# The opening of a two-layer trunk: a part's weight transfers ordered behind that part's last modulation row

## The chip, the cores and the metric

One core of one Trainium2 chip runs the whole program. The metric is the device time of one execution in microseconds (us); shown is the median over runs of the same kernel. The engines are TensorE (PE; PEld is its weight load), VectorE (DVE), ScalarE (ACT), GpSimd (POOL) and SyncE (SP), whose queue issues nearly all DMA transfers here.

## The reference

Two decoder layers on a sequence of 256 tokens with 2048 channels, in float32. Cut to what matters for this change:

```
cond = silu(c)
for l in range(2):
    mod = einsum('bd,de->be', cond, w_ada[l]) + b_ada[l]     # (1, 6 * 2048)
    sh_m, sc_m, gt_m, sh_f, sc_f, gt_f = six pieces of mod
    u = x * (1 + sc_m) + sh_m
    proj = u @ w_in[l]                                       # 4896 columns
    # sliding-window attention on one group of columns,
    # RWKV-7 delta rule on the others
    mix = concat(y_attn, y_rwkv) @ w_out[l]
    x = layer_norm(ALPHA * x + gt_m * mix)
    u = x * (1 + sc_f) + sh_f
    x = layer_norm(ALPHA * x + gt_f * swiglu(u))
```

So before the first projection can begin, the first two of the six modulation vectors of layer 0 have to be there: a product of one vector with 2048 x 4096 numbers of `w_ada`, that is 32 MB which are read once and used once.

## The kernel before, in words

The work of a layer is a mixer (input projection, attention, delta rule in four chunks of 64 tokens, output projection) and a feed-forward part. All weights are streamed from HBM. A float32 product is made of three matmuls: each weight tile `raw` is split into `hi` (a cast on ScalarE, L435) and `lo = raw - hi` (a subtraction on VectorE, L436), each input `u` into two halves as well, and hi x hi, hi x lo and lo x hi are summed. Weight tiles have 1024 columns in all and go through rings: four `raw`, three `hi`, two `lo` (`WB`).

*The opening* (some 150 us) is handled in five parts of 4, 4, 4, 2 and 2 of the 16 channel tiles of 128. For each part the generator `parts` (inside the last section of the kernel)

- streams 16 rows of `w_ada` through `ada_first`: row tiles `ast` of 128 x 1024 (512 KB; in the two small parts two rows of 256 KB share one), a ring of eight; VectorE multiplies each by a column of `cond` and adds it to `aacc` (L356 the first, L358 the others);
- sums `aacc` over its partitions in `ada_sums`: four transposes on TensorE (L327), a sum along the row on ScalarE for each (L331), and the bias on VectorE (`mods`, L334), once for the shift and once for the scale;
- makes the part's inputs in `make_u`: transposes of x (`xt`, L1372; TensorE L409), shift and scale on ScalarE (L413, L415), the low half on VectorE (L416);
- yields, and `front` runs `tstream` on the part's weight tiles: three kinds of columns (`rk`, `lb` and `acc`), matmuls L469 and L470 on `hi` and L471 on `lo`. The tiles come from `steps`, which issues the transfers (L427), the cast and the subtraction.

The opening uses one PSUM bank for transposes, so the sums and the transposes of x take turns. Later modulations (the other pieces of layer 0 and all of layer 1) are made beside the stream: `ada_steps` issues their rows through two buffers, adds them on VectorE (L268, L270) or multiplies them on TensorE (L290), and ends in an L327 too.

The order in which each engine runs its instructions is not that of the source: a planner simulates the program and lists the instructions of each engine by its own clock, subject to the data dependences and to hand-made order dependences that wait for nothing on the chip (`order`, `tc.add_manual_dep`: the second stands behind the first in the list). Within an engine everything then runs strictly in that list's order. All transfers are issued from SP's list; each waits there for the transfer eight before it, and for its buffer.

`lead` holds the name of the row transfer that `ada_first` issued last. It serves two helpers, `fetch` and `setup`, which put small parameter transfers behind it.

Of the kernel before, what the change touches and what calls it, by code (L numbers as in the profile page):

```python
# [69 lines left out]
def hybrid_trunk_kernel(  # L70
# [9 lines left out]
    dma = nc.sync.dma_start  # L80
# [11 lines left out]
    def bank(name="mb", tag="mb"):  # L92

        if tag == "cb":
            return ps.tile([P, 512], F32, tag="cb", name=name)
        t = f"m{turn[0]}"
        turn[0] ^= turn[1]
        return ps.tile([P, 512], F32, tag=t, name=name, bufs=1)
# [49 lines left out]
    order = mybir.DependencyInfo(mybir.DependencyClass.NoSync, mybir.DependencyReason.DATA)  # L148
# [23 lines left out]
    def fetch(dst, src, later=True):  # L172
        ins = dma(dst, src)
        if later:
            tc.add_manual_dep(ins.ins, lead[0], order, reason="behind the first modulation rows")
# [164 lines left out]
            S.copy(row, rb[0:n, 0:P])  # L340
            dma(gates[l, mod // 3, c0 // P:c0 // P + n], row)

    lead = []

    def ada_first(pool, c0, w):

# [36 lines left out]
    def pump():  # L383

        pace[1] += pace[0]
        while pace[1] >= 1.0:
            pace[1] -= 1.0
            next(ada_rest, None)
# [5 lines left out]
    def md(l, mod, kt, n=1):  # L394
        return mods[l][:, mod * KT + kt:mod * KT + kt + n]
# [23 lines left out]
    def steps(srcs, W, kts, room=None, off=0):  # L419


        no = max(1, 1024 // W)
        for i0 in range(0, len(kts), no):
            m = min(no, len(kts) - i0)
            raw = wp.tile([P, 1024], F32, tag="raw", name="raw", bufs=WB[0])
            for dst, src in srcs(raw[:, 0:m * W].rearrange("p (k w) -> p k w", w=W), kts[i0], m):
                dma(dst, src)  # L427
            if room:
                parts = [(raw[:, o * W:(o + 1) * W], *room()) for o in range(m)]
            else:  # L430
                hi = wp.tile([P, 1024 + WPAD], F32R, tag="hi", name="hi", bufs=WB[1])[:, off:off + 1024]
                lo = wp.tile([P, 1024 + WPAD], F32R, tag="lo", name="lo", bufs=WB[2])[:, off:off + 1024]
                parts = [(raw[:, 0:m * W], hi[:, 0:m * W], lo[:, 0:m * W])]
            for fl, h, r in parts:
                S.copy(h, fl)  # L435
                ins = V.tensor_tensor(r, fl, h.bitcast(F32), ALU.subtract)  # L436
            anchor[:] = [ins.ins.name]
            for o in range(m):
                if room:
                    yield i0 + o, *parts[o][1:]  # L440
                else:
                    yield i0 + o, hi[:, o * W:(o + 1) * W], lo[:, o * W:(o + 1) * W]
            pump()
# [42 lines left out]
    def cols(w, c0, width):  # L486
        wv = w.rearrange("(k p) n -> p k n", p=P)

        def f(rv, k0, m):
            return [(rv, wv[:, k0:k0 + m, c0:c0 + width])]  # L490
        return f
# [26 lines left out]
    def front(l, us, feeds, ahead=False):  # L518

        lb = [bank("lb", "cb") for _ in range(2)]  # L520
        vb = [acc_ps.tile([P, 512], F32, tag="acc", name="acc") for _ in range(4)]
        lblocks = [(0, 128, lb[0][:, 0:T], True, False), (128, 128, lb[0][:, T:2 * T], False, True),
                   (256, 32, lb[1][0:32, 0:T], not ahead, not ahead)]
        vblocks = [((2 * q + i) * P, P, vb[q][:, i * T:(i + 1) * T], i == 0, i == 1) for q in range(4) for i in range(2)]
        rk = None
        if ahead:
            b = ps.tile([P, 512], F32, tag="m1", name="rk0", bufs=1)
            turn[:] = 0, 0
            rk = [[b[:, 0:T], b[:, T:2 * T]], [lb[1][:, T:2 * T], None]]
            rblocks = [(0, P, rk[0][0], True, False), (P, P, rk[1][0], True, True), (2 * P, P, rk[0][1], False, True)]  # L530
            wrk = w_in[l][:, R0:R0 + 2 * RW].rearrange("(k p) (s n) -> p k s n", p=P, s=2)

            def rk_cols(rv, k0, m):
                return [(rv[:, :, 0:T], wrk[:, k0:k0 + m, 0, 0:T]), (rv[:, :, T:T + P], wrk[:, k0:k0 + m, 1, 0:P])]
        for kts, _ in feeds:
            fl = dict(first=kts[0] == 0, last=kts[-1] == KT - 1)
            if ahead and kts[0] == 0:
                tstream(rk_cols, T + P, kts, us, rblocks, **fl)
            tstream(cols(w_in[l], LORA0, 288), 288, kts, us, lblocks, **fl)
            if ahead and kts[0] > 0:  # L540
                tstream(rk_cols, T + P, kts, us, rblocks, **fl)
            tstream(cols(w_in[l], R0 + 2 * RW, RW), RW, kts, us, vblocks, **fl)
        return lb, vb, rk
# [814 lines left out]
    with tc.tile_pool(name="pro", bufs=1) as pp:  # L1358
        xv = x[0].rearrange("(t p) d -> p t d", p=P)

        def parts():
            k0 = 0
            for n in PARTS:
                o, w = k0 * P, n * P
                xt = pp.tile([P, 2, 512], F32, tag="xt", name="xt", bufs=2)[:, :, 0:w]
                side = setup(pp, 0, 0) if k0 == 0 else iter(())
                rows = ada_first(pp, o, w)
                for j in range(512 // w, KT + 1, 512 // w):
                    next(rows)
                    next(side, None)  # L1370
                    if j == 8:
                        dma(xt, xv[:, :, o:o + w])  # L1372
                for _ in side:
                    pass
                for _ in rows:
                    pass
                kts = list(range(k0, k0 + n))
                make_u(pp, [xt[:, 0, :], xt[:, 1, :]], k0, lambda kt: md(0, 1, kt), lambda kt: md(0, 0, kt), us, kts, IDLE["first"] if k0 + n == KT else 0)
                k0 += n
                yield kts, (0, 1)  # L1380
            for l, half in ((0, 1), (1, 0), (1, 1)):
                for _ in setup(pp, l, half, lead):
                    pass
            rope(pp)
            zt = pp.tile([P, 520], F32, name="zt")
            G.memset(zt, 0.0)
            for t in tinv:
                fetch(t.rearrange("e s t -> (e s t)").rearrange("(p n) -> p n", p=P), zt)
        feeds = front(0, us, parts(), ahead=True)
    for l in range(L):  # L1390
        pace[0] = AP[l]
        with tc.tile_pool(name=f"mix{l}", bufs=1, reuse_waits="tile") as mp:
            ys, wa = mixer(l, us, mp, feeds)
        pace[0] = AO[l]
        with tc.tile_pool(name=f"ffn{l}", bufs=1, reuse_waits="tile") as fp:
            us, feeds = channel(l, ys, wa, fp)
# [30 lines left out]
```

## Time and profile before

| | |
|---|---|
| median of 3 runs | 2643.07 us (2640.19 to 2645.76) |
| the profiled execution by its own time | 2641.74 us |
| its span | 2640.0 us |
| TensorE busy in the span | 2499.2 us (95%) |
| VectorE busy | 1803.9 us (68%) |
| ScalarE busy | 1185.9 us (45%) |
| the opening's rows and weights (issued before 128 us) | 46.50 MB at a mean of 363 GB/s |

How to read the profile's lines. In the timeline each line is a start, a duration, an engine, a source line, the operation, output <- inputs with their shapes, a count, and in brackets how long the engine stood idle before it and what ended that. In the table by stretches each engine has its busy time (with its count), then the granted TensorE clock (1.00 is full), the mean busy share of the core's 16 DMA engines and the rate in GB/s.

### The profile page before, as it was taken

How to read it: one execution, taken by the hardware profiler on the slowest of the kernel's cores; microseconds unless marked ns; L12 is line 12 of the kernel's file. 1: busy time of each engine (PE TensorE's matmuls, PEld its weight loads, DVE VectorE, ACT ScalarE, POOL GpSimd, SP SyncE). 2: the span in 40 equal slices, each digit the busy share in tenths (PEclk: the TensorE clock that was granted, in tenths of full speed). 3: DMA queues.
4: the chain of work that ended last, by engine and by line, in shares of the span. 5: the costliest groups of instructions: out<-in, count | busy, mean ns of one | idle time of the engine just before them, and what ended most of it. 6: DMA issues, size and time to landing. Idle time of an engine off the chain costs nothing.

```text
span 2640.0 us, 42213 instructions
## 1 busy us (share of the span) xinstructions
PE 2499.2 (95%) x15619; PEld 2081.6 (79%) x15619; DVE 1803.9 (68%) x2439; ACT 1185.9 (45%) x2023; POOL 144.1 (5%) x368
## 2 busy tenths in 40 slices
PE   3799998999999999999999989989899999999997
PEld 3797785677888888888898977867788888888887
DVE  7977666579877787777887776565755455545456
ACT  2464454435544444444454545544444443344442
POOL 1002222000000000000000024110000000000000
PEclk9899999999999999999999999989999999999999
DMA  9988667698998888888878784415665655566654
GB/s 371 343 267 256 195 187 250 224 357 290 339 329 307 312 314 312 287 311 296 300 240 282 219 262 147 130 51 210 211 199 186 191 188 193 194 190 190 191 188 147
DMA packets 336383, 637.50 MB, mean 241 GB/s; under 512 B 59510, under 2 KB 126514, under 8 KB 334642
## 3 DMA queue, kind: packets, MB, share of 16 engines
q1 hardware_dynamic: 333170, 629.05, 71.1%
q0 software_dynamic: 1280, 2.62, 0.4%
q10 hardware_dynamic: 1728, 3.15, 0.3%
q8 instruction: 122, 2.00, 0.3%
q14 instruction: 83, 0.68, 0.1%
HBM read 622.08 MB, written 12.62 MB: 240 GB/s over the span
## 4 chain that ended last, share of the span: by engine, by line
PE 80%; DMA 10%; DVE 7%; issue 2%; ACT 1%; SPq 0%; POOL 0%; DVEq 0%; ACTq 0%; POOLq 0%
PE acc L458 21%; PE acc L457 20%; PE acc L460 20%; DMA ast<-in_w_ada_dram 5%; PE acc L471 2%; PE acc L469 2%; PE acc L470 2%; DVE lo L436 2%; DMA raw<-in_w_in_dram 1%; DVE aacc L270 1%; DMA raw<-in_w_out_dram 1%; DVE aacc L358 1%; PE mb L1296 1%; PE mb L327 1%; PE gv L290 1%
## 5 line engine op out<-in xcount | busy, mean ns | idle before, releaser
L436 DVE TENSOR_TENSOR lo<-raw,hi 128x1024 fp32r<-128x1024 f32 (+2 forms) x728 | 881.3, 1211 | 556.7 <-PE acc L458 378.2
L435 ACT CAST hi<-raw 128x1024 fp32r<-128x1024 f32 (+2 forms) x728 | 758.2, 1044 | 1051.8 <-PE acc L460 831.0
L458 PE MATMUL acc<-lo,u 128*128 128x512 f32 x1568 | 514.8, 396 | 8.5 <-DVE lo L436 8.5
L460 PE MATMUL acc<-hi,u 128*128 128x512 f32 x1568 | 508.1, 393 | 0.0
L457 PE MATMUL acc<-hi,u 128*128 128x512 f32 x1568 | 460.0, 395 | 2.0 <-ACT sg L1289 1.2
L270 DVE SCALAR_TENSOR_TENSOR aacc<-ast,cond,aacc 128x1024 f32<-128x1024 f32 x270 | 344.9, 1277 | 39.5 <-DMA ast<-in_w_ada_dram 39.0
L458 PEld LDWEIGHTS acc<-lo,u 128*128 128x128 f32 x1568 | 295.2, 189 | 71.6 <-DVE lo L436 10.9
L457 PEld LDWEIGHTS acc<-hi,u 128*128 128x128 f32 x1568 | 296.1, 189 | 65.1 <-ACT sg L1289 1.6
L460 PEld LDWEIGHTS acc<-hi,u 128*128 128x128 f32 x1568 | 296.7, 189 | 61.7
L458 PE MATMUL acc<-lo,ht 128*128 128x512 f32 (+1 forms) x720 | 243.3, 377 | 1.6 <-DVE lo L436 1.6
L460 PE MATMUL acc<-hi,ht 128*128 128x512 f32 (+1 forms) x720 | 242.2, 375 | 0.0
L457 PE MATMUL acc<-hi,ht 128*128 128x512 f32 (+1 forms) x720 | 217.0, 376 | 0.0
L469 PE MATMUL acc<-u,hi 128*128 128x256 f32 x720 | 201.5, 287 | 1.9 <-ACT hi L435 1.9
L470 PE MATMUL acc<-u,hi 128*128 128x256 f32 x720 | 200.5, 286 | 0.0
L471 PE MATMUL acc<-u,lo 128*128 128x256 f32 x720 | 189.9, 290 | 7.1 <-DVE lo L436 6.9
L458 PEld LDWEIGHTS acc<-lo,ht 128*128 128x128 f32 x720 | 135.1, 188 | 27.0 <-DVE lo L436 3.1
L460 PEld LDWEIGHTS acc<-hi,ht 128*128 128x128 f32 x720 | 135.6, 188 | 24.3
L457 PEld LDWEIGHTS acc<-hi,ht 128*128 128x128 f32 x720 | 134.8, 188 | 24.3
L469 PEld LDWEIGHTS acc<-u,hi 128*128 128x128 f32 x720 | 139.9, 194 | 5.8 <-ACT hi L435 2.3
L470 PEld LDWEIGHTS acc<-u,hi 128*128 128x128 f32 x720 | 139.5, 194 | 2.8 <-issue 1.7
L471 PEld LDWEIGHTS acc<-u,lo 128*128 128x128 f32 x720 | 131.2, 194 | 12.1 <-DVE lo L436 9.0
L1135 POOL TENSOR_TENSOR brs<-brs,mhalf 128x1 f32<-128x1 f32 x8 | 6.2, 785 | 1687.4 <-DVE brs L1134 766.8
(358 smaller groups left out, 2900.7 us busy)
## 6 DMA issues: line engine op xcount, KB each, us to landing
ast<-in_w_ada_dram SPq DMA_DIRECT2D x368, 512.0 KB
raw<-in_w_gate_up_dram SPq DMA_DIRECT2D x704, 256.0 KB
raw<-in_w_down_dram SPq DMA_DIRECT2D x176, 512.0 KB
raw<-in_w_in_dram SPq DMA_DIRECT2D x82, 512.0 KB
raw<-in_w_out_dram SPq DMA_DIRECT2D x64, 512.0 KB
raw<-in_w_in_dram SPq DMA_DIRECT2D x120, 256.0 KB
ast<-in_w_ada_dram SPq DMA_DIRECT2D x32, 256.0 KB
lnw<-in_ln_w_dram SPq DMA_DIRECT2D x4, 1024.0 KB
```

Source lines behind the costliest of these rows:

```text
L270: ins = V.scalar_tensor_tensor(acc, t, cond[:, j:j + 1], acc, ALU.mult, ALU.add)
L290: PE.matmul(gv[32 * q:32 * q + 32, 0:T], lhsT=cond[:, j:j + 1].to_broadcast([P, 32]), rhs=t[:, q * T:(q + 1) * T], start=(j == 0), stop=(j ...
L327: PE.transpose(b[:, i * P:(i + 1) * P], blocks[q + i], ident)
L358: V.scalar_tensor_tensor(acc, t[:, j], cond[:, j0 + j:j0 + j + 1], acc, ALU.mult, ALU.add)
L435: S.copy(h, fl)
L436: ins = V.tensor_tensor(r, fl, h.bitcast(F32), ALU.subtract)
L457: PE.matmul(bt, lhsT=xh, rhs=hi[:, c0:c0 + w], start=st, stop=False)
L458: PE.matmul(bt, lhsT=xh, rhs=lo[:, c0:c0 + w], start=False, stop=False)
L460: PE.matmul(banks[t][q][:, 0:w], lhsT=xl, rhs=hi[:, c0:c0 + w], start=False, stop=sp_)
L469: PE.matmul(bt, lhsT=hi[:, c0:c0 + w], rhs=xh, start=st and opens, stop=False)
L470: PE.matmul(bt, lhsT=hi[:, c0:c0 + w], rhs=xl, start=False, stop=False)
L471: PE.matmul(bt, lhsT=lo[:, c0:c0 + w], rhs=xh, start=False, stop=sp_ and closes)
```

## The change

The weight transfers that `steps` issues while the opening is built get an order dependence on `lead[0]`, the last row transfer of the part that is in hand. A flag, `opening`, is true around the call of `front` that builds the opening and false afterwards. No instruction, no byte and no wait is added; the planner's lists change.

```
--- before.py
+++ after.py
-    lead = []
+    lead, opening = [], [False]
...
             for dst, src in srcs(raw[:, 0:m * W].rearrange("p (k w) -> p k w", w=W), kts[i0], m):
-                dma(dst, src)
+                ins = dma(dst, src)
+                if opening[0]:
+                    tc.add_manual_dep(ins.ins, lead[0], order, reason="behind the modulation rows of the part")
...
+        opening[0] = True
         feeds = front(0, us, parts(), ahead=True)
+        opening[0] = False
```

What moves is seen in the lists. Lines behind L427 are two higher after the change (L436 becomes L438, L469 to L471 become L471 to L473), those in the last section more.

The first place is SP's list in part 0. `ast` are rows, `raw` weights, `xt` a piece of x, `posi` the positions; the part's last row is ast_213. Before:

```order
L353 DMA ast_195<-in_w_ada_dram 128x2x512
L427 DMA raw_268<-in_w_in_dram 128x2x256
L353 DMA ast_198<-in_w_ada_dram 128x2x512
L427 DMA raw_268<-in_w_in_dram 128x2x128
L427 DMA raw_293<-in_w_in_dram 128x2x256
L353 DMA ast_201<-in_w_ada_dram 128x2x512
L427 DMA raw_293<-in_w_in_dram 128x2x128
L427 DMA raw_318<-in_w_in_dram 128x3x288
L353 DMA ast_204<-in_w_ada_dram 128x2x512
L427 DMA raw_351<-in_w_in_dram 128x288
L1372 DMA xt_486<-in_x_dram 128x2x512
L353 DMA ast_207<-in_w_ada_dram 128x2x512
```

The same place after the change, from the row transfer ast_204 on:

```order
L353 DMA ast_204<-in_w_ada_dram 128x2x512
L353 DMA ast_207<-in_w_ada_dram 128x2x512
L353 DMA ast_210<-in_w_ada_dram 128x2x512
L353 DMA ast_213<-in_w_ada_dram 128x2x512
L427 DMA raw_268<-in_w_in_dram 128x2x256
L427 DMA raw_268<-in_w_in_dram 128x2x128
L427 DMA raw_293<-in_w_in_dram 128x2x256
L427 DMA raw_293<-in_w_in_dram 128x2x128
L427 DMA raw_318<-in_w_in_dram 128x3x288
L427 DMA raw_351<-in_w_in_dram 128x288
L353 DMA ast_488<-in_w_ada_dram 128x2x512
```

The six weight transfers stand behind all sixteen rows, and the next part's first row (ast_488) behind them; on VectorE the subtractions of raw_268 and raw_293 likewise moved from between the rows to behind them. Over the whole opening the same transfers stand ahead of the last row.

The second place is VectorE's list where part 2's rows end and part 3's begin (aacc_1129, row pairs ast_1130, ast_1135, ...); lo_750 and lo_780 are weight tiles of part 1. Before:

```order
L358 SCALAR_TENSOR_TENSOR aacc_808<-ast_855,cond_131,aacc_808 128x1024
L356 TENSOR_SCALAR aacc_1129<-ast_1130,cond_131 128x2x256
L358 SCALAR_TENSOR_TENSOR aacc_1129<-ast_1130,cond_131,aacc_1129 128x2x256
L436 TENSOR_TENSOR lo_750<-raw_747,hi_749 128x1024
L334 SCALAR_TENSOR_TENSOR mods0_127<-asum_858,par0_123 128x4
L358 SCALAR_TENSOR_TENSOR aacc_1129<-ast_1135,cond_131,aacc_1129 128x2x256
L436 TENSOR_TENSOR lo_780<-raw_777,hi_779 128x1024
```

And after:

```order
L358 SCALAR_TENSOR_TENSOR aacc_808<-ast_855,cond_131,aacc_808 128x1024
L438 TENSOR_TENSOR lo_750<-raw_747,hi_749 128x1024
L356 TENSOR_SCALAR aacc_1129<-ast_1130,cond_131 128x2x256
L438 TENSOR_TENSOR lo_780<-raw_777,hi_779 128x1024
L358 SCALAR_TENSOR_TENSOR aacc_1129<-ast_1130,cond_131,aacc_1129 128x2x256
L334 SCALAR_TENSOR_TENSOR mods0_127<-asum_858,par0_123 128x4
```

The two weight tiles moved ahead of row work of part 3, as their transfers did on SP ahead of ast_1130's pair.

The third place is TensorE's list at the end of the opening, where the rows of part 4 end: mb_1353 are the transposes of its sums (aacc_1310), hi_1070 and lo_1071 a weight tile of part 2. Before:

```order
L469 MATMUL acc_155<-u_892,hi_1040 128x256
L470 MATMUL acc_155<-u_892,hi_1040 128x256
L471 MATMUL acc_155<-u_892,lo_1041 128x256
L327 MATMUL mb_1353<-ident_75,aacc_1310 128x128 x2
L469 MATMUL acc_152<-u_902,hi_1070 128x256
L470 MATMUL acc_152<-u_902,hi_1070 128x256
L469 MATMUL acc_153<-u_902,hi_1070 128x256
```

And after:

```order
L473 MATMUL acc_155<-u_892,lo_1041 128x256
L471 MATMUL acc_152<-u_902,hi_1070 128x256
L472 MATMUL acc_152<-u_902,hi_1070 128x256
L471 MATMUL acc_153<-u_902,hi_1070 128x256
L472 MATMUL acc_153<-u_902,hi_1070 128x256
L471 MATMUL acc_154<-u_902,hi_1070 128x256
L472 MATMUL acc_154<-u_902,hi_1070 128x256
L471 MATMUL acc_155<-u_902,hi_1070 128x256
L472 MATMUL acc_155<-u_902,hi_1070 128x256
L327 MATMUL mb_1353<-ident_75,aacc_1310 128x128 x2
L473 MATMUL acc_152<-u_902,lo_1071 128x256
```

The eight matmuls on hi_1070 moved ahead of the transposes; those on lo_1071 stay behind them. Further on in the same list the transposes of part 4's x (L409, mb_1366) moved from 40 weight matmuls ahead of the first matmul that uses their result (u_1373) to directly ahead of it.

In the mixer of layer 0 the lists differ as well. Weight matmuls stand 20 to 70 places earlier against the operations of the delta rule; between one pair of L806 groups of its inversion there are 28 weight matmuls now and 60 before. The rows of aacc_3833 (a later modulation) begin two weight tiles later on VectorE, and behind the subtraction lo_5601 nine of the sixteen are left, against seven before. From layer 0's feed-forward part on the lists are nearly the same.

## The prediction

> **What bounds the kernel now.** I read the page's engine table and chain first, then a table by stage, then the timeline of the opening, because the edit acts there and nowhere else by itself.
>
> ```profile
> span 2640.0 us, 42213 instructions
> PE 2499.2 (95%) x15619; PEld 2081.6 (79%) x15619; DVE 1803.9 (68%) x2439; ACT 1185.9 (45%) x2023; POOL 144.1 (5%) x368
> PE 80%; DMA 10%; DVE 7%; issue 2%; ACT 1%; SPq 0%; POOL 0%; DVEq 0%; ACTq 0%; POOLq 0%
> ```
>
> TensorE is busy for 2499.2 of 2640.0 us, so only the 141 us in which it stands idle can be won. The stages, with PE, PE weight loads, DVE, ACT and POOL busy time, then the granted clock, the DMA share and GB/s:
>
> ```profile
> 20.00:40.00 20.00, 2.31 (x9) 1.51 (x10) 15.49 (x28) 5.65 (x21) 0.00 (x0) 1.00 1.06 392
> ...
> 30.00:58.00 28.00, 18.18 (x120) 16.15 (x121) 24.46 (x38) 9.48 (x29) 0.00 (x0) 1.00 1.04 392
> 58.00:94.00 36.00, 27.01 (x204) 25.67 (x204) 34.67 (x37) 13.70 (x32) 0.00 (x0) 0.89 1.06 392
> 94.00:128.00 34.00, 25.69 (x192) 23.40 (x190) 31.50 (x50) 17.64 (x45) 0.00 (x0) 0.90 0.99 325
> ...
> 160.00:260.00 100.00, 94.23 (x842) 83.74 (x842) 79.78 (x127) 52.43 (x107) 18.63 (x35) 0.95 0.83 262
> 360.00:460.00 100.00, 87.78 (x931) 62.93 (x930) 77.26 (x169) 44.66 (x121) 17.38 (x39) 0.95 0.82 259
> ```
>
> From 20 to 128 us DMA (0.99 to 1.06 of its engines) and VectorE (90.63 of 98 us from 30 to 128) are both full, TensorE is not. After 160 TensorE is the bound, with stalls of some us in the mixer. So the question is whether anything gained in the opening reaches 128 us, and what the new order does to the mixer.
>
> **The change part by part.** No instruction and no byte is added. First the modulation rows of part 0, which now go ahead of that part's six weight transfers (2 of 256 KB, 2 of 128 KB, 432 KB, 144 KB: 1344 KB). The timeline of before:
>
> ```profile
> 29.90 1.28 DVE L358 SCALAR_TENSOR_TENSOR aacc<-ast,cond,aacc 128x1024 f32<-128x1024 f32 x1 [1.85 <-DMA ast<-in_w_ada_dram]
> ...
> 34.32 1.12 PE L327 MATMUL mb<-ident,aacc 128*128 128x128 f32 x4 [19.06 <-DVE aacc L358]
> ...
> 39.90 0.16 DVE L334 SCALAR_TENSOR_TENSOR mods<-asum,par 128x4 f32<-128x4 f32 x1 [0.86 <-ACT mb L331]
> ...
> 42.13 0.42 DVE L416 TENSOR_TENSOR u<-uf,u 128x256 fp32r<-128x256 f32 x1 [0.87 <-ACT u L415]
> 42.15 0.58 PE L469 MATMUL rk<-u,hi 128*128 128x256 f32 x1 [1.11 <-ACT u L415]
> ...
> 112.56 0.94 DVE L436 TENSOR_TENSOR lo<-raw,hi 128x768 fp32r<-128x768 f32 x1
> ```
>
> 1344 KB are 1.376 MB; at 392 GB/s (the 20:40 row) that is 3.5 us. The last rows wait for DMA (1.85 us at 29.90), so they end 3.5 us sooner, and two subtractions of 0.94 us each (the last row above is of that shape) no longer stand between them. The transposes then begin at about 30.6 instead of 34.32. From there to the first matmul took 42.15 - 34.32 = 7.8 us; ACT now has a cast or two of the moved weights in between (1.04 us for a wider one, at 124.40 below), so I give it 8.4 to 9.0, and the first matmul comes at 39.0 to 39.6: 2.6 to 3.2 us sooner. The moved weights land 3.5 us behind the last row, near 32.5, well ahead of that. VectorE has the same work behind it at its first L416 and fewer waits, so it too is up to 2.8 us ahead.
>
> Does that last? TensorE is idle a quarter of the time until 128, so it needs rows, and rows need DMA and VectorE. The last wait of VectorE before the end of the opening is this:
>
> ```profile
> 96.58 1.22 DVE L436 TENSOR_TENSOR lo<-raw,hi 128x1024 fp32r<-128x1024 f32 x1 [1.88 <-ACT hi L435]
> 96.60 0.58 PE L469 MATMUL acc<-u,hi 128*128 128x256 f32 x1 [1.85 <-ACT hi L435]
> ...
> L353 SPq DMA_DIRECT2D ast<-in_w_ada_dram x80: 367/368/748, 1.3 to 117.0; - x80
> ```
>
> At 96.58 VectorE and TensorE wait together for a weight tile's cast, that is for a landing. In the new order that tile stands one row pair (512 KB, 1.3 us at 392 GB/s) further ahead and the row pair behind it: by 96.6 the same bytes must have come in. VectorE then reaches 96.6 with its work changed by one pair against one tile (1.23 against 1.22 us), and from there to 129.20 it has no gap over 0.2 us. So I take the head start as eaten here: 0. The bounds are -2.8 us (all kept: the last row was issued at 117.0 and used 10 us later, so the ring would allow it) and +1.0 (a row pair waited for where a tile was).
>
> Second, the end of the opening. Rows of before, then TensorE in two stretches:
>
> ```profile
> 123.39 4.68 DVE L358 SCALAR_TENSOR_TENSOR aacc<-ast,cond,aacc 128x512 f32<-128x512 f32 x6
> ...
> 124.40 1.04 ACT L435 CAST hi<-raw 128x1024 fp32r<-128x1024 f32 x1 [2.88 <-DMA raw<-in_w_in_dram]
> ...
> 127.98 1.22 DVE L436 TENSOR_TENSOR lo<-raw,hi 128x1024 fp32r<-128x1024 f32 x1
> ...
> 128.21 0.66 PE L327 MATMUL mb<-ident,aacc 128*128 128x128 f32 x2 [3.93 <-DVE aacc L358]
> ...
> 130.38 0.41 PE L471 MATMUL acc<-u,lo 128*128 128x256 f32 x1
> ...
> 142.12 0.60 PE L409 MATMUL mb<-ident,xt 128*128 128x128 f32 x4
> ...
> 143.57 0.56 ACT L415 ACTIVATE u<-mb,mods 128x256 fp32r<-128x256 f32 x1
> ```
>
> ```profile
> 130.00:135.00 5.00, 5.00 (x29) 5.00 (x29) 2.16 (x4) 1.94 (x5) 0.00 (x0) 0.62 0.89 265
> 135.00:140.00 5.00, 5.00 (x46) 4.96 (x45) 1.62 (x2) 0.03 (x1) 0.00 (x0) 1.00 1.00 367
> ```
>
> Before, TensorE stood 3.93 us for the transposes of part 4's sums although hi_1070 was cast by 125.44; its eight matmuls came behind, until 130.38. Now those eight stand ahead of the transposes. lo_1071 is ready at 127.98 + 1.22 = 129.20, so the first L471 comes at 129.20, not 130.38: -1.2 us. The idle time falls into two pieces, 1.4 us until 125.4 and 1.7 us from 126.3 to 128.0. After 3.93 us the clock was 0.62, and 29 matmuls went in 5 us where 46 go at full clock: 17 x 5/46 = 1.85 us lost. What gaps do to the clock here:
>
> ```profile
> 63.84 0.39 PE L471 MATMUL acc<-u,lo 128*128 128x256 f32 x1 [2.73 <-DVE lo L436]
> ...
> 93.66 1.09 PE L327 MATMUL mb<-ident,aacc 128*128 128x128 f32 x4 [2.96 <-DVE aacc L358]
> ```
>
> ```profile
> 93.00:96.00 3.00, 1.09 (x4) 0.72 (x4) 1.66 (x3) 1.13 (x5) 0.00 (x0) 0.50 1.09 366
> 62.00:65.00 3.00, 1.16 (x9) 1.17 (x10) 3.00 (x4) 1.04 (x1) 0.00 (x0) 1.00 1.07 390
> ```
>
> A gap of 2.73 us left the clock at 1.00, one of 2.96 us was followed by 0.50. Two gaps of 1.4 and 1.7 us should leave it whole: between 0 and -1.85; I take -1.5, since 0.7 us of waiting for lo_1071 could come near enough to join the two. The Trainium skill ("TensorE: Matmul & The Clock Gate", Part 1: The HAM clock gate) has the array drop to half rate after an idle window of about 3.4 us, and ask as long a busy one to return. The gap of 2.96 us speaks for a shorter limit here; by the page's figure this term would be an estimated -1.7, by the rows it is -1.85, so the sum hardly depends on which holds.
>
> Against it, the transposes of part 4's inputs (L409, 142.12) had 40 weight matmuls between them and the first use of their result; now that use follows at once. The result was ready at 143.57 + 0.56 = 144.13, and L409 ended at 142.72: +1.4 us, with bounds 0 (if the weights are late anyway) and 1.4. Opening: -1.2 - 1.5 + 1.4 = -1.3, between -5.9 (all of the head start and of the clock, and no L409 wait) and +2.4 (the bad bound of the head start, neither gain).
>
> Third, the mixer of layer 0. The planner places weight matmuls 20 to 70 earlier against the chain of the delta rule, and row work of the later modulations later. Rows of before:
>
> ```profile
> 375.79 0.39 PE L457 MATMUL acc<-hi,u 128*128 128x512 f32 x1
> 376.01 0.39 PE L458 MATMUL acc<-lo,u 128*128 128x512 f32 x1
> ...
> 388.90 0.67 DVE L814 TENSOR_TENSOR tm<-tm,m 128x512 f32<-128x512 f32 x1
> ...
> 391.83 0.69 DVE L802 STREAM_TRANSPOSE ytr<-tm 128x512 f32<-128x512 f32 x1
> ...
> 399.70 1.28 DVE L270 SCALAR_TENSOR_TENSOR aacc<-ast,cond,aacc 128x1024 f32<-128x1024 f32 x1
> ...
> 412.83 1.28 DVE L270 SCALAR_TENSOR_TENSOR aacc<-ast,cond,aacc 128x1024 f32<-128x1024 f32 x1 [2.38 <-DMA ast<-in_w_ada_dram]
> ...
> 415.84 1.09 PE L327 MATMUL mb<-ident,aacc 128*128 128x128 f32 x4 [5.28 <-DVE aacc L270]
> ```
>
> One step of the inversion (L813 to the next L806) loses its weight matmuls: 0.67 + 0.69 = 1.4 us uncovered, 2.7 if a row of 1.28 us is ahead in VectorE's queue. At 415.84 TensorE waits 5.28 us for a sum whose last rows come one per (412.83 - 399.70)/4 = 3.3 us, by DMA. Behind the last weight tile of that stretch seven of them were left, now nine: +6.6 us if that tile comes no sooner, about 0 if it comes 7 us sooner: 32 of its matmuls, 0.22 us apart (375.79, 376.01), that now run before one step of the inversion instead of behind it. The other way, more weights ahead of the chain means its inputs are older when it reads them: the idle time of the two stages quoted above, 5.8 and 12.2 us, could shrink; I allow -4. Between -4 and 6.6 + 1.4 = +8 I take +1.5, near the step that surely loses its cover, and count the row wait as mostly absorbed in the 5.28 us that are waited already. The feed-forward stages keep their order: 0.
>
> The sum is -1.3 + 1.5 = +0.2 us. The profiled run took 2641.74 us by its own time (1.7 more than its span) and lies 1.3 under the median 2643.07; the shift is applied to the median: **2643.3 us**.
>
> **The rivals.** *The head start is kept (faster).* VectorE is 2.8 us ahead at its first L416 and never pays it back, so 128.21 becomes 125.4 and the clock stays up. For it: the last row was issued 10 us before its use. Against it: the wait at 96.58. Opening -1.2 - 1.85 - 2.8 + 1.4 = -4.5, and the mixer at -2 instead of +1.5: 2636.6.
>
> *The sums of the next modulation come late (slower).* Two rows more behind the last weight tile, 3.3 us each, at the L327 that already waits 5.28 us; it decides when that wait passes 5.28 + 1.5. With the uncovered step: -1.3 + 6.6 + 1.4 = +6.7: 2649.8. For it: rows there come by DMA alone. Against it: earlier weight tiles start the rows' clock earlier.
>
> *Weights come too late to their matmuls (slightly slower).* A part's tiles behind its rows would be missed at each hand-over as at 96.60, 1.85 us; if the last parts repeat it once more at 128 and the order gains nothing: +1.4 + 1.85 = +3.3: 2646.4. In part 0 the tiles have some 6 us to spare. The Trainium skill ("Trainium Kernel Development and Optimization", Best Practices) advises double buffering so that transfers overlap compute, which speaks against fetching weights later; in this trace transfers overlap in either order, DMA being full.
>
> *Nothing lasting happens:* head start and tail both vanish, 2643.
>
> **How the numbers follow.** About 0.2%, 5.3 us, is what a measurement of this kernel can tell from no change. Forecast 0.44 (its own range 2638 to 2648), kept head start 0.22, late sums 0.20, late weights 0.08, nothing 0.06. Faster by over 5.3 us needs 2637.8: most of the kept head start (0.18) and an edge of the forecast (0.04), 0.22. Slower needs 2648.4: most of the late sums (0.18), some of the late weights and of the forecast's edge (0.05), 0.23. The rest is 0.55. The range reaches from the kept head start, 2636, to the late sums with the opening's bad bound, 2652.
>
> **What would show it.** Right: part 0's transposes near 30.6 and first matmul near 39.3; VectorE and TensorE together near 96 and 128 as before; the eight hi_1070 matmuls before the L327 at 128; full clock from 130 to 135; an idle of about 1.4 us behind the last L409. Wrong: the L327 at 126 or sooner, the clock still near 0.62, the wait of the L327 at 415.84 over 7 us, or other stalls in the mixer that move the end by over 5 us.

## The result and the profile after

| | before | after |
|---|---|---|
| median of 5 runs each, same chip | 2644.46 us (2640.19 to 2647.40) | 2682.18 us (2674.20 to 2687.67) |
| ratio, 95% interval | | 1.0146 (1.0134 to 1.0158) |
| the profiled execution by its own time | 2641.74 us | 2687.67 us |
| its span | 2640.0 us | 2686.0 us |

The kernel is 38 us slower, far outside the forecast range. The profiled execution of after is the slowest of its five runs, so the two spans differ by 46 us rather than 38. The engine table of after:

```profile
span 2686.0 us, 42209 instructions
PE 2523.2 (94%) x15619; PEld 2097.8 (78%) x15619; DVE 1807.7 (67%) x2439; ACT 1187.4 (44%) x2023; POOL 144.8 (5%) x368
```

The same 15619 matmuls took 2523.2 us instead of 2499.2. That is 24 us more of busy time for equal work, which speaks for a lower clock: the mean granted clock of the two profiled executions is 0.978 and 0.969, and 2499.2 * 0.978 / 0.969 is 2522. The other 22 of the 46 us are idle time. Where the two lie is seen in the stretches of the mixers, each with equal work: layer 0's and then layer 1's, first of before and then of after (columns as in the prediction).

```profile
159.03:605.20 446.17, 418.15 (x3744) 333.09 (x3744) 317.59 (x577) 205.52 (x460) 63.89 (x148) 0.97 0.77 249
1364.09:1885.83 521.74, 489.00 (x4207) 412.93 (x4205) 359.31 (x642) 257.73 (x529) 68.68 (x151) 0.96 0.60 189
```

```profile
162.91:636.38 473.47, 437.22 (x3745) 347.74 (x3745) 321.32 (x579) 206.69 (x461) 64.50 (x148) 0.92 0.72 235
1394.91:1931.47 536.56, 491.92 (x4207) 413.05 (x4205) 359.82 (x642) 257.94 (x529) 67.50 (x151) 0.96 0.58 184
```

In layer 0's mixer TensorE stands idle for 36.2 us instead of 28.0 and is busy for 19 us longer, with the clock at 0.92 instead of 0.97. In layer 1's mixer it is idle for 44.6 us instead of 32.7 and busy for 3 us longer.

The opening, in TensorE's timeline of after:

```profile
31.09 1.11 PE L327 MATMUL mb<-ident,aacc 128*128 128x128 f32 x4 [15.73 <-DVE aacc L358]
...
40.17 0.58 PE L471 MATMUL rk<-u,hi 128*128 128x256 f32 x1 [1.11 <-ACT u L415]
...
59.06 0.38 PE L471 MATMUL acc<-u,hi 128*128 128x256 f32 x1 [2.56 <-ACT hi L437]
...
61.36 0.58 PE L473 MATMUL acc<-u,lo 128*128 128x256 f32 x1 [1.10 <-DVE lo L438]
...
67.60 0.60 PE L327 MATMUL mb<-ident,aacc 128*128 128x128 f32 x4
...
74.45 0.80 PE L471 MATMUL lb<-u,hi 128*128 128x256 f32 x2 [1.11 <-ACT u L415]
...
95.47 1.08 PE L327 MATMUL mb<-ident,aacc 128*128 128x128 f32 x4 [4.37 <-DVE aacc L358]
...
126.08 0.38 PE L471 MATMUL acc<-u,hi 128*128 128x256 f32 x1 [1.12 <-ACT hi L437]
...
130.38 0.66 PE L327 MATMUL mb<-ident,aacc 128*128 128x128 f32 x2 [3.10 <-DVE aacc L358]
131.43 0.58 PE L473 MATMUL acc<-u,lo 128*128 128x256 f32 x1 [0.39 <-DVE lo L438]
...
150.57 0.50 PE L471 MATMUL lb<-u,hi 128*128 128x256 f32 x2 [1.54 <-ACT u L415]
```

Against the same operations of before:

```profile
59.92 0.38 PE L469 MATMUL acc<-u,hi 128*128 128x256 f32 x1
...
65.83 0.60 PE L327 MATMUL mb<-ident,aacc 128*128 128x128 f32 x4
...
73.60 0.79 PE L469 MATMUL lb<-u,hi 128*128 128x256 f32 x2 [1.43 <-ACT u L415]
```

Part 0 is 3.2 us ahead at its transposes (31.09 against 34.32) and 2.0 at its first matmul (40.17 against 42.15). At 59.06 the lead is 0.86 us: TensorE had waited for a weight tile's cast, and the cast for the tile's transfer (ScalarE in after):

```profile
57.97 1.04 ACT L437 CAST hi<-raw 128x1024 fp32r<-128x1024 f32 x1 [6.95 <-DMA raw<-in_w_in_dram]
```

At the transposes of part 1's sums the lead has turned into 1.8 us of lag (67.60 against 65.83). From part 0's first weight matmul to these transposes, in before and then in after:

```profile
42.15:65.83 23.68, 19.93 (x149) 18.83 (x149) 22.06 (x23) 7.28 (x11) 0.00 (x0) 1.00 1.05 391
```

```profile
40.17:67.60 27.43, 23.76 (x173) 23.11 (x174) 25.15 (x26) 8.77 (x13) 0.00 (x0) 0.94 1.05 395
```

TensorE stands idle for some 3.7 us in both, but its new list has 24 weight matmuls more ahead of the transposes, and the clock is lower. What follows these transposes is late in turn. That shows in VectorE's waits from 58 to 94 us (total, times, longest) for the steps by which ScalarE makes a part's modulation and inputs, of before and then of after:

```profile
DVE u L416 <- ACT u L415: 0.4, 1, 0.4
```

```profile
DVE u L416 <- ACT u L415: 2.0, 2, 1.1
DVE mods L334 <- ACT mb L331: 1.0, 1, 1.0
```

0.4 us have become 3.0. At the L327 near 95 the lag is 1.8 (95.47 against 93.66), at that of part 4 2.2 (130.38 against 128.21), and layer 0's mixer begins 3.9 us late (162.91 against 159.03). From 130 to 135 us the clock is 0.50, where 0.62 had been:

```profile
130.00:135.00 5.00, 4.23 (x18) 3.87 (x19) 2.73 (x6) 0.73 (x4) 0.00 (x0) 0.50 0.73 219
```

The opening isn't where 38 us went.

The mixer of layer 0, first as waits of TensorE between 340 and 530 us (total, times, longest). Before, and then after:

```profile
PE mb L327 <- DVE aacc L270: 5.3, 1, 5.3
PE gv L290 <- DMA ast<-in_w_ada_dram: 2.4, 3, 1.6
```

```profile
PE gv L290 <- DMA ast<-in_w_ada_dram: 7.8, 5, 2.8
PE ta L828 <- DVE tm L816: 5.9, 2, 5.7
PE db L880 <- DVE rh L859: 5.0, 2, 3.2
...
PE mb L327 <- DVE aacc L270: 0.2, 1, 0.2
```

The wait of L327 that the prediction watched is gone. In its place TensorE waits for `tm`, a step of the inversion (0.8 us in before), for `rh`, and longer for rows. What held `tm` up stands in VectorE's timeline of after, and when its operand was there in TensorE's:

```profile
425.37 1.28 DVE L270 SCALAR_TENSOR_TENSOR aacc<-ast,cond,aacc 128x1024 f32<-128x1024 f32 x1 [1.58 <-DMA ast<-in_w_ada_dram]
428.89 1.28 DVE L270 SCALAR_TENSOR_TENSOR aacc<-ast,cond,aacc 128x1024 f32<-128x1024 f32 x1 [2.23 <-DMA ast<-in_w_ada_dram]
430.09 0.68 DVE L816 TENSOR_TENSOR tm<-tm,m 128x512 f32<-128x512 f32 x1
```

```profile
421.95 1.67 PE L815 MATMUL m<-tm,yx 64*64 64x64 f32 x32
...
430.82 1.43 PE L828 MATMUL ta<-atl,tm 64*64 64x64 f32 x21 [5.66 <-DVE tm L816]
```

The product `m` was complete by 423.62. `tm` takes 0.68 us and could have followed, but VectorE's list has two more rows ahead of it, and each waits for its landing, one per 3 us. Between 423.78 us, when it ended the row before these, and 430.09 VectorE stands idle for 1.58 + 2.23 = 3.81 us with `tm` behind the row that it waits for. TensorE has no weight matmul there to fill the gap. The idle is followed by a low clock for a long time (a stretch of after):

```profile
430.00:450.00 20.00, 17.01 (x143) 12.01 (x145) 9.34 (x19) 5.20 (x22) 11.56 (x31) 0.50 0.62 198
```

From 430 to 450 the clock is half. Layer 1 has a second loss, mostly idle time as the stretches above show. The lag of after against before at the start of each stage (the first `ssb`, the first transposes of the feed-forward part, of layer 1, of layer 1's feed-forward part) is 3.9, 31.2, 30.8 and 45.6 us in these two profiles. So the opening gave 3.9 us, the mixer of layer 0 27.3, its feed-forward part -0.4, the mixer of layer 1 14.8, and what came behind that is 0.4.

Why layer 1 at all, when the edit acts on the first 30 us? Compared by name, the lists of all engines but GpSimd differ there too: 144 of 697 VectorE instructions and TensorE's by up to 44 places. The planner works in one pass with its own clock, and the opening shifted everything behind it. With the dependence in part 0 alone, or on the four `rk` transfers alone, all lists are those of after; with it in parts 1 to 4 alone, all lists are those of before. The only transfers that it moves by itself are the kernel's first six of weights; the rest is the planner's redraw.

### The profile page after: what moved, and what is told of

Same layout as the page of the kernel before. It is cut to its first block, busy times and chain, and to the rows that moved or that the text cites. A ratio compares the mean times of both kernels' runs of the same rounds, so it can differ in the third digit from the quotient of the medians.

```text
span 2686.0 us, 42209 instructions
## 1 busy us (share of the span) xinstructions
PE 2523.2 (94%) x15619; PEld 2097.8 (78%) x15619; DVE 1807.7 (67%) x2439; ACT 1187.4 (44%) x2023; POOL 144.8 (5%) x368
## 4 chain that ended last, share of the span: by engine, by line
PE 73%; DMA 6%; DVE 4%; POOL 1%; ACT 1%; issue 1%; SPq 0%; DVEq 0%; ACTq 0%; POOLq 0%
PE acc L460 20%; PE acc L462 20%; PE acc L459 20%; PE acc L473 2%; PE acc L471 2%; PE acc L472 2%; DMA ast<-in_w_ada_dram 1%; DMA raw<-in_w_out_dram 1%; DVE lo L438 1%; PE mb L1298 1%; PE gv L290 1%; POOL tmp L792 1%; PE mb L327 1%; POOL ttl L794 0%; DMA nscr<-am 0%
## 5 line engine op out<-in xcount | busy, mean ns | idle before, releaser
L438 DVE TENSOR_TENSOR lo<-raw,hi 128x1024 fp32r<-128x1024 f32 (+2 forms) x728 | 882.2, 1213 | 567.3 <-PE acc L460 386.1
L471 PE MATMUL acc<-u,hi 128*128 128x256 f32 x720 | 202.6, 289 | 3.7 <-ACT hi L437 3.7
L473 PE MATMUL acc<-u,lo 128*128 128x256 f32 x720 | 190.5, 292 | 3.6 <-DVE lo L438 3.6
L471 PEld LDWEIGHTS acc<-u,hi 128*128 128x128 f32 x720 | 141.4, 197 | 7.9 <-ACT hi L437 4.1
L473 PEld LDWEIGHTS acc<-u,lo 128*128 128x128 f32 x720 | 133.0, 197 | 8.6 <-DVE lo L438 5.6
```

The costliest lines, as they stand in the source:

```text
L471: PE.matmul(bt, lhsT=hi[:, c0:c0 + w], rhs=xh, start=st and opens, stop=False)
L473: PE.matmul(bt, lhsT=lo[:, c0:c0 + w], rhs=xh, start=False, stop=sp_ and closes)
```

## The experiments

The theory after this reading: the loss is in the lists of the two mixers, and the opening itself costs some 4 us. The rival: the opening is at fault, and the mixers only pass its lateness and its clock on. What separates them is to hold one kernel's lists while the other's opening runs. This is done at the end of the kernel, from a table of the other kernel's instructions on each engine, from the start of layer 0's mixer on or for one layer or one engine only:

```
+    for row in <the other kernel's list of each engine>:
+        for a, b in zip(row, row[1:]):
+            tc.add_manual_dep(named[b], a, order, reason="the list of the other kernel")
```

These are the same order dependences as those of the change; no wait and no instruction comes in. Every ratio below is against executions of the kernel before that were taken alongside.

**1. After's opening, before's lists from layer 0's mixer on.** The edit: the table above in the kernel after, with before's lists.

> The opening as changed; from the first instruction of layer 0's mixer on, each engine keeps the order that it had before the change. Theory A (the loss of 38 us lies in the lists of the two mixers, which the planner drew anew): the opening alone ends 2 to 4 us later, as in the profiles (the transposes of part 4 at 130.4 instead of 128.2), and the rest runs as before, so 2646 to 2649. Theory B (the changed opening hands on something that costs later whatever the lists, such as late tiles, rings out of step or a cold clock): at least half of the loss stays, 2663 or more. Theory C (the opening really gains, as its head start would have it): 2640 or less.

Measured: 2649.06 us against 2644.64, ratio 1.0014 (1.0002 to 1.0026). The opening alone costs 4 us, between 1 and 7, which agrees with the 3.9 us of lag in the profile. 33 of the 38 us go with the lists.

**2. Before's opening, after's lists.** The edit: the kernel before with after's lists from layer 0's mixer on.

> The mirror: the opening as before, from layer 0's mixer on the order that the changed kernel has. Theory A: nearly the whole loss, 2676 to 2682, with the wait of some 5 us at the inversion's last step of the first group near 430. Theory B: 2655 or less.

Measured: 2670.92 us, 1.0100 (1.0084 to 1.0116): 26 us, under the expected 2676 to 2682. The lists cost the larger part by themselves, but 26 and 4 make 30 and not 38. What the two do to each other isn't explained by this pair.

**3. After, with layer 1's lists of before.** The edit: the table for layer 1 alone in the kernel after.

> The changed kernel, but from layer 1's projection on the order of before. The profiles put 31 us of the loss ahead of 1396 us and 15 behind it. Theory A, both mixers by their lists: 2666 to 2670. Rival: the 15 us of layer 1 belong to that one profiled run (it was the slowest of five, 5.5 us over the median) and not to its list, in which few instructions moved: 2676 to 2682.

Measured: 2665.13 us, 1.0081 (1.0060 to 1.0102), a microsecond under the first range and far from the rival's. Layer 1's lists are worth 17 us, and what remains, 20 us, is the opening's 4 and layer 0's.

**4. After, with VectorE's list of before.** The edit: the table for VectorE alone, from layer 0's mixer on.

> The changed kernel with VectorE alone held to its order of before from layer 0's mixer on; the planner draws the other engines' lists around that. Theory D (in the changed mixer VectorE's list has rows of the next modulation, which come by DMA every 3 us, ahead of steps of the inversion, and TensorE waits for these steps): most of the loss goes, 2645 to 2655. Rival E (TensorE's list is the cause, its weight matmuls being used up ahead of the chain): TensorE's list stays partly as changed, so a third or more of the loss stays, 2657 or more.

Measured: 2663.50 us, 1.0066 (1.0049 to 1.0083). Half of the loss goes, half stays: theory D missed its range, and the number lies in rival E's. In its profile the wait for `tm` is gone from the list of waits, but the rows are still waited for (TensorE, 340 to 530 us):

```profile
PE gv L290 <- DMA ast<-in_w_ada_dram: 7.9, 8, 1.6
PE mb L327 <- DVE aacc L270: 5.7, 1, 5.7
```

The L327 waited 5.3 us in before as well; what is new against before is the 7.9 us at L290. By stage (table at the end of this section) layer 1's mixer adds 2.6 us in this profile and layer 0's 14.7, so what went is mostly layer 1's loss. The planner has redrawn TensorE's list around VectorE's, and it is neither kernel's, so the run doesn't price VectorE's order alone. That led to the question of whether the order or the rows' transfers are the cause, layer by layer.

**5. Before, with layer 0's lists of after.** The edit: the table for layer 0 alone in the kernel before.

> The kernel before, but each engine's list for layer 0 (from its mixer to its last matmul) is that of the changed kernel; opening and layer 1 as before. It prices layer 0's list alone: the run with both layers' lists cost 26 us, of which the profiles put 13 in layer 1, so some 13 are expected: 2653 to 2662. If it costs under 5, layer 0's loss needs the changed opening ahead of it.

Measured: 2664.21 us against 2647.98, 1.0060 (1.0047 to 1.0073): 16 us, 3 more than expected. The waits show the same picture as after's, with before's opening ahead of it:

```profile
PE gv L290 <- DMA ast<-in_w_ada_dram: 6.3, 7, 1.5
PE ta L826 <- DVE tm L814: 5.6, 2, 5.4
```

**6 and 7. The rows of layer 0's mixer with a quarter of the bytes, with before's and with after's lists.** Of each row tile only 256 of its 1024 columns are transferred, and VectorE and TensorE read them four times; three quarters of those modulations' weights are left out. Every operation keeps its size and its place. Cut to the rows that VectorE adds; those that TensorE multiplies are cut down in the same way.

```
-            fetch(t, src[:, j, n0:n0 + 1024], j < 2 and not done)
+            w = 256 if pace[0] == AP[0] else 1024
+            fetch(t[:, 0:w], src[:, j, n0:n0 + w], j < 2 and not done)
+            tq = t[:, 0:w].rearrange("p (o n) -> p o n", o=1).to_broadcast([P, 1024 // w, w]) if w < 1024 else t
```

> The kernel before with its lists held, but the modulation rows that are fetched beside layer 0's mixer bring a quarter of their bytes (256 of 1024 columns; VectorE and TensorE read that quarter four times over, so their work is the same, and a part of the transfer is left out). It is the base for the next run. All theories: the waits for rows in the mixer go (5.3 us ahead of one L327, 2.4 us ahead of L290, and what the rows hold up on VectorE), so 2625 to 2640.

Measured: 2632.89 us, 0.9945 (0.9931 to 0.9959), 15 us less than before.

> Layer 0's list of the changed kernel, the rest as before, and the rows beside layer 0's mixer quartered as in the run on the base. Theory D (in that list steps of the inversion stand in VectorE's queue behind rows that come by DMA one per 3 us): with fast rows the two lists cost the same within 4 us, so 4 us or less above the base with quartered rows. Rival E (TensorE's weight matmuls are used up ahead of the chain, so each step of the chain is waited for whatever the rows do): most of the 13 us stays, 9 us or more above that base.

Measured: 2636.80 us, 0.9953 (0.9935 to 0.9970). With the rows' bytes there, after's lists in layer 0 cost 16 us; with a quarter of them 3.9 us by the medians, and the two intervals overlap. Layer 0's mixer as a whole, of number 5, then of 6 and of 7:

```profile
159.86:627.68 467.82, 433.05 (x3744) 344.15 (x3745) 320.58 (x579) 206.15 (x460) 63.52 (x148) 0.93 0.73 237
```

```profile
158.91:599.52 440.61, 420.05 (x3744) 336.49 (x3744) 318.49 (x577) 206.75 (x460) 67.40 (x148) 0.95 0.57 177
```

```profile
160.68:602.92 442.24, 422.01 (x3744) 337.23 (x3744) 319.74 (x579) 206.02 (x460) 64.42 (x148) 0.95 0.56 177
```

With whole rows after's list leaves TensorE idle for 34.8 us, where before's left it 28.0; with small rows the two lists leave 20.2 and 20.6, at the same clock. Single waits don't all go, though. In number 7 that at L290 is gone, that for `tm` is shorter, and that for `rh`, 4.3 us in number 5, is not:

```profile
PE db L882 <- DVE rh L861: 5.2, 2, 3.3
PE ta L830 <- DVE tm L818: 3.4, 2, 3.2
```

So layer 0's loss needs both, after's list and rows that land late. Which of the waits carries how much of it isn't shown. The rows' bytes also load the DMA engines for everything else; whether it is the landing of the rows themselves or that load, this pair can't tell, though the waits above name the rows.

**8. After, with TensorE's list of before.** The edit: the table for TensorE alone, both layers.

> The changed kernel with TensorE alone held to its order of before from layer 0's mixer on; the planner draws the other lists around that and comes near those of before (50 of VectorE's 435 instructions of the mixer stand elsewhere, by 7 places at most). Rival E: 2648 to 2655, that is lower than the 2663.5 with VectorE held. Theory D alone: 2655 or more, since rows still may stand ahead of steps.

Measured: 2666.34 us, 1.0072 (1.0057 to 1.0087). The rival, that the earlier weight matmuls on TensorE are what costs, missed by over 10 us: half of the loss stays, as it did with VectorE's list. In its profile `tm` costs 0.7 us, and the L327 waits again:

```profile
PE mb L327 <- DVE aacc L270: 5.9, 1, 5.9
...
PE ta L828 <- DVE tm L816: 0.7, 1, 0.7
```

Both are waits of before (5.3 and 0.8), so they are no part of the loss. By stage layer 1's mixer adds 2.8 us here and layer 0's 13.5. What stays in layer 0 isn't found: TensorE's idle time in that mixer is 30.0 us, where number 1 has 29.4, and the clock is 0.94, where number 1 has 0.95.

**9. Before, with layer 1's lists of after.** The edit: the table for layer 1 alone in the kernel before.

> The kernel before, with the changed kernel's lists in layer 1 alone (from its projection on; few instructions moved there, on VectorE 144 of 697 by 17 places at most). The run with both layers' lists cost 26 us and layer 0's alone 16, so 10 are expected, 13 by the stage times: 2655 to 2662. If it costs under 4, layer 1's loss only comes on top of a loss in layer 0.

Measured: 2664.04 us against 2646.20, 1.0070 (1.0053 to 1.0088): 18 us, more than the 10 to 13 expected. The opening's 4, layer 0's 16 and this 18 make 38, as measured; but see number 2 for the two layers together.

**10 and 11. The rows of layer 1's mixer with a quarter of the bytes, with before's and with after's lists.** The edit is that of 6 and 7, for layer 1.

> The kernel before with its lists held and a quarter of the bytes in the modulation rows beside layer 1's mixer (the rest of the transfer is left out, the work on VectorE and TensorE is not). The base for the next run. The transfers are idle most of the time from 1660 to 1860 us, so little can be gained: 2636 to 2648.

Measured: 2643.78 us, 0.9989 (0.9978 to 1.0000).

> Layer 1's lists of the changed kernel with layer 1's rows quartered. Theory D for layer 1 too (rows ahead of the chain): within 4 us of the base with quartered rows. Rival F (in layer 1 it is VectorE's order of softmax and inversion, the steps L814 and L802 standing 8 to 10 places later and the softmax 11 sooner): 8 us or more above that base.

Measured: 2662.46 us, 1.0059 (1.0041 to 1.0078). After's lists in layer 1 cost as much with the smaller rows, 18.7 us, as with the whole ones. In layer 1 the rows are not the cause; that fits rival F, which names VectorE's order instead.

**12. After, with the smaller rows in both mixers.** The edit is that of 6 and 7, for both layers, in the kernel after with its own lists.

> The changed kernel with its lists held and the rows beside both mixers quartered. If rows are layer 0's loss, the opening costs 4 us and layer 1 keeps its loss, the sum is the base with quartered rows (2633) + 4 + 4 + 10 = 2651, with 2646 to 2656. If the opening's late hand-over made the rows matter, 2643 or less. If the rows explain only what they did with the opening of before, 2660 or more.

Measured: 2650.64 us, 1.0017 (1.0004 to 1.0029), as expected: 31.5 us less than after. Before's 2646.20, the -15 and -2 of smaller rows, the opening's 4, 4 for layer 0 and 18 for layer 1 make 2655; the sum holds within 5 us. The expected sum had 10 for layer 1, where number 9 measured 18, so that it came so close is in part luck.

**13 and 14. Before, with after's list in layer 1 on VectorE alone, and on TensorE alone.** The edit: the table for layer 1 and one engine.

> The kernel before, in layer 1 VectorE alone held to its order in the changed kernel; the planner draws the other engines' lists around it. Layer 1's whole set of lists costs 18 us. Theory F (VectorE's order of softmax and inversion is the cause): 12 us or more of them come with VectorE's order alone. Rival G (the loss needs the lists of several engines together): 6 us or less.

Measured: 2655.85 us against 2645.73, 1.0040 (1.0022 to 1.0058).

> The same with TensorE alone held to its order in the changed kernel (557 of its instructions in layer 1 stand elsewhere, by 44 places at most). Theory F: 6 us or less. Rival H (TensorE's list is what the time hangs on, the other engines follow it): 12 us or more. Rival G: 6 us or less in this one and the other.

Measured: 2656.27 us, 1.0042 (1.0021 to 1.0063). Each gives 10 us, more than theory G and less than F and H had, so none of the three holds. Neither engine's list carries the 18 us alone. The waits of TensorE between 1560 and 1860 us, of before and of all lists of after (number 9):

```profile
PE m L806 <- DVE den L1005: 3.8, 1, 3.8
...
PE db L878 <- DVE rh L857: 2.3, 1, 2.3
...
PE acc L963 <- DVE mx L989: 0.6, 1, 0.6
```

```profile
PE db L878 <- DVE rh L857: 5.7, 2, 3.1
PE acc L963 <- DVE mx L989: 4.8, 1, 4.8
```

The wait for `den` is gone from the list, and those for `rh` and `mx` are longer, both steps of the attention or of the delta rule. In 13 the planner draws a new list for TensorE, in 14 for VectorE, and it is neither kernel's, so 10 and 10 may hold mismatches of their own. Mixing them the other way, VectorE's list of before among after's others in layer 1 alone, wasn't tried. Which step of layer 1's lists costs most stays open.

**15. The dependence on two of the six transfers.** The last question was whether the loss grows with the change to the opening.

```
-                if opening[0]:
+                if opening[0] and W == 288:
```

> The change for two of part 0's six transfers alone (the tiles of 288 columns). The opening's lists come out between the two kernels', while all lists from layer 0's mixer on are those of the changed kernel, instruction by instruction. Theory A: 2670 to 2685, as those lists cost 26 us behind the opening of before and 38 behind the changed one. Rival: the loss hangs on the opening, and half of the change costs half or less: 2664 or less.

Measured: 2679.47 us, 1.0132 (1.0113 to 1.0151). Only the two transfers of the 288-column weights are ordered, the opening's lists lie between before's and after's, and from the mixer on all lists are those of after. The loss comes whole, 34 of the 38 us.

The lag by stage in the profiled runs tells the same, roughly. In microseconds against the profile of before:

| | at layer 0's mixer | added in it | added in layer 1's mixer |
|---|---|---|---|
| after | 3.9 | 27.3 | 14.8 |
| 1: before's lists | 5.2 | 5.3 | -2.7 |
| 2: before's opening | 0.5 | 17.8 | 12.8 |
| 3: layer 1's lists of before | 2.9 | 21.3 | -0.3 |
| 4: VectorE's list of before | 3.7 | 14.7 | 2.6 |
| 5: before, layer 0's lists of after | 0.8 | 21.7 | 0.7 |
| 8: TensorE's list of before | 3.6 | 13.5 | 2.8 |
| 9: before, layer 1's lists of after | 0.5 | 9.2 | 12.4 |
| 15: two of the six transfers | 5.3 | 14.5 | 16.3 |

Row 9 shows how far one profile can be trusted: its layer 0 has before's lists and is 9.2 us slower there. The six profiles with before's lists and whole rows in layer 0's mixer (1, 9, 10, 11, 13, 14) are 2.8 to 12.1 us slower in it than the profile of before, at clocks of 0.94 to 0.96 against its 0.97; so that profile came out short there, and after's 27.3 is too large a price. In layer 1's mixer the profiles with before's lists (1, 3, 5, 6, 7, 10) lie between -5.2 and 1.4, those with after's (after, 2, 9, 11, 12, 15) between 11.2 and 16.3. The verdicts above rest on the medians.

No version came out that beats the kernel before with the whole computation; the change is a loss. A third buffer for the rows wasn't tried.

## Why the prediction was wrong, point by point

*The head start of part 0.* Right in kind: 31.09 for 30.6 at the transposes, 40.17 for 39.0 to 39.6 at the first matmul. It was said to be eaten at 96, by a landing. A landing did take 1.1 us of it, but at 59, and the rest was gone at 67.60: TensorE's new list has 24 weight matmuls more ahead of the transposes of part 1's sums, a change of order that the prediction had not looked at. The wait at 96.58 on which it built was not shown to be for a landing either. In ScalarE's list of before that cast, at 95.51, stands behind two sums, and ScalarE had stood idle until the transposes for them:

```profile
94.84 0.26 ACT L331 ACTIVATE mb<-mb 128x128 f32<-128x128 f32 x1 [10.60 <-PE mb L327]
```

The L327 at 95.47 waited 4.37 us where it had waited 2.96. The term was 0 with a bad bound of +1.0; measured at the last L327, it was +2.2.

*The eight matmuls and the clock.* They did go ahead of the L327, at 126.08. But the idle pieces are 1.12 and 3.10 us and not 1.4 and 1.7, because the sums came 2.2 us late. L473 began at 131.43 and not at 129.20. The first gain, -1.2, held against the L327: 1.05 us lie between it and the first matmul on lo_1071, where 2.17 had lain; it was covered by the 2.2 us of lag. The second, -1.5, failed on the head start's term: the matmuls were moved into the gap, but the gap's end moved too, and the clock from 130 to 135 was 0.50, where 0.62 had been and 1.00 was forecast. On the limit, the row of 2.96 us was the one to trust: 3.10 us of idle were enough. The Trainium skill ("TensorE: Matmul & The Clock Gate", Part 1: The HAM clock gate) has the clock fall after an idle window of about 3.4 us; the trace, with 3.10 us here and 2.96 in before, does not agree.

*The transposes of part 4's x.* +1.4 forecast, 1.54 us measured.

*The opening's sum.* -1.3 forecast, between -5.9 and +2.4; 4 us measured by experiment 1 and 3.9 in the profile.

*The mixer of layer 0: the step that failed first.* It was "One step of the inversion (L813 to the next L806) loses its weight matmuls: 0.67 + 0.69 = 1.4 us uncovered, 2.7 if a row of 1.28 us is ahead in VectorE's queue", with +1.5 taken and +8 as the bound. The place was right and the size was not. A row in VectorE's queue was priced at its execution, 1.28 us, although the same paragraph had its arrival, one per 3.3 us. `tm` stood behind rows still on their way, and the wait was 5.66 us. The prediction put the 3.3 us at the L327 instead, where the wait fell from 5.28 to 0.23. What such a gap does to the clock behind it was counted in the opening, and not here, where 20 us at half clock followed it. Experiment 5 measured the term at 16 us, with before's opening ahead of it, and 7 showed that it needs the rows' bytes. How much of the 16 us is this one wait for `tm`, and how much those for `rh` and at L290, no run separates. In the profiles most of it is busy time at a lower clock, 19 of 27 us in after.

*The mixer of layer 1: the step that was left out.* The sum has no term for it; the text went from layer 0's mixer to "The feed-forward stages keep their order: 0." That sentence held (-0.4 us over layer 0's, 0.4 behind layer 1's mixer), but the lists of layer 1's mixer had changed, and were passed over as nearly the same. Experiment 9 measured 18 us.

*The rivals.* "The sums of the next modulation come late" had the right cause in layer 0, rows that come by DMA alone, at the wrong place, and 2649.8 for 2682. The head start that is kept is refuted by the L327 at 130.38. Late weights cost some of the head start, at 59.06. At the hand-overs that this rival named they don't show: near 96 TensorE no longer waits for a cast, and the cast that it waits for at 126.08, 1.12 us, came behind ScalarE's inputs of part 3 and not behind a landing.

*What stays open.* Both mixers' lists behind before's opening cost 26 us, while 16 and 18, measured one at a time, make 34, and 38 less the opening's 4 is as much. Executions of one program differ by 10 us and more, and the intervals of such sums are 5 us wide or more, but that was not shown to be the reason. The 18 us that stay in each of 4 and 8, of which the opening has 4, aren't explained either. Which steps carry layer 1's 18 us isn't settled either.

## What to carry to other kernels

Where a planner lists the engines, an order dependence is a change to every list behind it: compare the whole lists by name, price each stage that differs, and expect a result that is not in proportion to the edit. On an engine that runs strictly in order, an instruction that is fed by a transfer costs those behind it the time until its data land, not its own duration; look for chain steps behind such rows. And price an idle gap together with the lower clock behind it.

## What the runs showed of the hardware

The granted clock fell to 0.50 after an idle of 3.10 us at 130.38, and had done so after 2.96 us in before, while 2.73 us left it at 1.00. In after's opening two shorter gaps were followed by a low clock too, 2.56 us at 59.06 and 1.10 us at 61.36 with eight matmuls between them. And the clock did not come back while TensorE was busy without a gap, with small matmuls for the most part. The two stretches of after:

```profile
61.00:65.00 4.00, 3.64 (x18) 3.64 (x19) 3.83 (x4) 1.58 (x3) 0.00 (x0) 0.57 1.05 388
```

```profile
436.00:445.00 9.00, 9.00 (x60) 5.69 (x58) 2.49 (x5) 2.43 (x10) 5.41 (x18) 0.50 0.60 178
```

So the length of one idle isn't all that decides, nor is busy time as the profile counts it; no run here isolated the rule. This bears on the prediction too, which took two gaps of 1.4 and 1.7 us to be harmless because each is under 2.73.
